# Fixing VectorE's instruction order over the middle stage of a decoder trunk: one step of convolution, recurrence or block sums behind each product's sums

## Chip, cores and metric

The kernel runs on one core of a Trainium2 chip. The metric is device time in microseconds (us), lower is better. The engines named below are PE (TensorE), DVE (VectorE), ACT (ScalarE), POOL (GpSimd) and SP (SyncE, which issues the DMA transfers).

## The reference

One decoder layer for 1024 tokens of width 1024 in float32. The part that matters here is the token-mixing sub-layer: one wide projection `u = h @ w_in` gives the inputs of three branches and their gates, and one of the branches is a recurrence over the tokens.

```python
u = h @ w_in[l]
dq, dk, dv, rq, rk, rv, rg, lx, ly, gates = split(u)
xc = causal_conv4(lx, conv_w) + conv_b            # per channel
r = sigmoid(xc @ w_a + b_a); i = sigmoid(xc @ w_x + b_x)   # 8 blocks of 128
a = exp(-8 * r * softplus(-lam))
b = sqrt(1 - a * a) * (i * xc)
hl[t] = a[t] * hl[t - 1] + b[t]                   # the recurrence (scan)
o_l = hl * gelu(ly)
o_r = silu(rg) * retention_output
merged = sum over 3 branches of sigmoid(gate_i) * (o_i @ w_branch[i])
```

After it come the output projection, cross-attention and the MLP.

## The kernel before

Every float32 operand is split into a high and a low part (`split`, L68: ACT casts the high part, DVE or POOL subtracts to get the low part), and each product is three matmuls (`mm3`). The large products use a seven-product block scheme: a weight pair is two units of 128 output channels, halved into blocks A11 to A22; DVE forms four sums of blocks (`left`, L1115) and two low parts (`prepare` for k = 1, 2), POOL the other five low parts; the right side is the blocks of h. One pair is seven products (`ORDER` = 1, 2, 6, 7, 5, 4, 3, called slots 0 to 6 here) of 12 matmuls into one PSUM tile each; `product` (L1161) then adds the PSUM results into the four output blocks, which is seven PSUM reads by DVE and one copy by ACT. PSUM holds six such tiles (`bufs=6`). `self.line` is a queue of preparations: each product first calls `ahead`, which prepares the unit of the product three further on.

The change is in `h_products` (L647). It goes through 23 pairs: pairs 2, 4, ..., 16 are the eight LRU blocks (`lx` and `ly`), between them stand two `rg` pairs (3 and 5) and then gate pairs. Around an LRU pair p:

- `lru_conv` is four DVE steps over 1024 elements, after slot 5 of pair p;
- `lru_split` and `lru_gate` follow in slots 5 and 6 of pair p + 1: the gate's 12 matmuls write `psr` and `psi`, ACT makes the sigmoids into tiles `r` and `g`, POOL multiplies, ACT does tanh, exp and sqrt, and DVE does four recurrence steps (L638 to L641; the third is the scan);
- `o_sums` loads two row blocks of a branch's output into tiles that share the tags `r` and `g`, makes four subtractions on DVE, and stores them for the next stage. Pair 4 has one set of these sums, pairs 6, 8, 10 and 14 have two, pair 12 one, pairs 18 and 20 one.

Tiles `r` and `g` have one buffer each. So the order of use is gate, recurrence, sums (twice in pairs with two sets), next gate, and each waits until the one before has let go: the sums' load waits for the scan and the last step, the second set's load for the first set's stores to land, and the next sigmoids for the last set's stores.

Nothing fixes the order on DVE except the data and a few `after` chains: a planner places every instruction on its engine by program order and its own estimate of when operands are ready. On the chip each engine then runs its list in that order.

Of the kernel before, what the change touches and what calls it, by code (L numbers as in the profile page):

```python
# [2 lines left out]

# [6 lines left out]
F32 = mybir.dt.float32  # L10
F32R = mybir.dt.float32r
AF = mybir.ActivationFunctionType
ALU = mybir.AluOpType
# [4 lines left out]
P = 128  # L18
S = 1024
D = 1024  # L20
KT = 8
HB = 512
# [5 lines left out]
V_CW = 1  # L28
V_CB = V_CW + 32
# [10 lines left out]
class Split:  # L40


    def __init__(self, hi, lo):
        self.hi, self.lo = hi, lo
# [2 lines left out]
        return Split(self.hi[key], self.lo[key])  # L47


class Kernel:  # L50
    def __init__(self, tc, a, out, ctx):
        self.tc, self.nc, self.a, self.out, self.ctx = tc, tc.nc, a, out, ctx
        self.last, self.put_off, self.filled = {}, [], None
        self.sp = self.sps = None

# [550 lines left out]
        self.split(s, st, self.nc.gpsimd)  # L606
        return s[:, 0, :], s[:, 1, :]

    def lru_conv(self, n, c, sp):
        nc, lx = self.nc, c["lx"]  # L610
        col = lambda base, t=0: self.vec[:, base + 8 * t + n:base + 8 * t + n + 1]
        xc = c["xc"] = sp.tile([P, S], F32, tag="xc", name="xc")
        nc.vector.tensor_scalar(xc, lx[:, 0:S], col(V_CW, 0), col(V_CB), op0=ALU.mult, op1=ALU.add)
        for t in range(1, 4):
            nc.vector.scalar_tensor_tensor(xc, lx[:, t:t + S], col(V_CW, t), xc, op0=ALU.mult, op1=ALU.add)

    def lru_split(self, c):
        xs = self.wpool.tile([P, 2, S], F32R, tag="w", name="xcs")
# [3 lines left out]
    def lru_gate(self, n, c, sp, sps):  # L622
        nc = self.nc
        col = lambda base: self.vec[:, base + n:base + n + 1]
        lw = self.lru_weights(n, sp)
        xc, gy, xs = c["xc"], c["gy"], c["xs"]
        r, g = (sp.tile([P, S], F32, tag=t, name=t) for t in "rg")
        for dst, w, vb in ((r, lw[0], V_BA), (g, lw[1], V_BX)):
            for half in range(2):
                sl = slice(half * HB, (half + 1) * HB)  # L630
                ps = self.ps.tile([P, HB], F32, tag="mm", name="psr") if dst is r else sps.tile([P, HB], F32, tag="p", name="psi", bufs=6)
                self.mm3(ps, w, xs[:, sl], True, True)
                nc.scalar.activation(dst[:, sl], ps, AF.Sigmoid, bias=col(vb))
        nc.gpsimd.tensor_tensor(xc, g, xc, op=ALU.mult)
        nc.scalar.activation(g, r, AF.Tanh, scale=self.sp4[:, n:n + 1])
        nc.scalar.activation(r, r, AF.Exp, scale=self.spm8[:, n:n + 1])
        nc.scalar.activation(g, g, AF.Sqrt)
        nc.vector.scalar_tensor_tensor(g, r, 1.0, g, op0=ALU.add, op1=ALU.mult)  # L638
        nc.vector.tensor_tensor(xc, xc, g, op=ALU.mult)
        nc.vector.tensor_tensor_scan(g, r, xc, 0.0, op0=ALU.mult, op1=ALU.add)  # L640
        nc.vector.tensor_tensor(gy, gy, g, op=ALU.mult)  # L641
        nc.sync.dma_start(self.olT[n * P:(n + 1) * P, :], gy)

    def l4(self, sp):
        return sp.tile([P, S], F32, tag="l4", name="l4", bufs=3)
# [1 line left out]
    def h_products(self):  # L647


        nc, v, a = self.nc, self.nc.vector, self.a  # L650
# [3 lines left out]
        jobs = [("rg", n) for n in range(4)] + [("gate", n) for n in range(self.n_gates, 24, 2)]  # L654
        for n in range(8):
            jobs.insert(2 + 2 * n, ("lru", n))
        cs, m = [{} for _ in jobs], len(jobs)

        sums = {4: [(0, 0)], 6: [(1, 0), (1, 1)], 8: [(1, 2), (1, 3)], 10: [(0, 1), (0, 2)], 12: [(0, 3)],
                14: [(2, 0), (2, 1)], 18: [(2, 2)], 20: [(2, 3)]}  # L660
# [4 lines left out]
        self.bcs = [[{} for _ in range(4)] for _ in range(3)]  # L665
        for i, b in zip((1, 0, 2), self.bcs):
            pairs += [(b[p], [a["w_br"][i * 8 + 2 * p + e] for e in range(2)]) for p in range(4)]

        def prep(p, k):
            self.pair_load(p, *pairs[p])  # L670
            self.prepare(k, pairs[p][0], v if p >= m and k in (6, 4) else nc.gpsimd)

            turns = [x for x in (0, m - 2, m + 2, m + 6, m + 10) if x <= p < x + 2]
            q, at = (p + 1, 6) if not turns else (turns[0] + 2, 3 if p > 1 else 4)
            if k == at and p == (turns or [p])[0] and q < len(pairs):
                self.pair_load(q, *pairs[q])
# [8 lines left out]
        def run(p, k):  # L685
            (kind, n), c, sp, sps = jobs[p], cs[p], self.sp, self.sps
            self.ahead()
            if kind == "lru" and k == 1:
                c["lx"], c["gy"] = sp.tile([P, S + 3], F32, tag="lx", name="lx"), self.l4(sp)
                nc.gpsimd.memset(c["lx"][:, 0:3], 0.0)  # L690

            def emit(i, j, x, y):
                tt = lambda o, x, y, op=ALU.add: v.tensor_tensor(o, x, y, op=op)
                sl = slice(j * HB, (j + 1) * HB)
                if kind == "lru":
                    if i == 1:
                        tt(c["lx"][:, 3 + j * HB:3 + (j + 1) * HB], x, y)
                    else:
                        tt(c["gy"][:, sl], x, y)
                        nc.scalar.activation(c["gy"][:, sl], c["gy"][:, sl], AF.Gelu_apprx_tanh)  # L700
                    return
                o = self.l4(sp)
                row = slice((2 * n + i) * P, (2 * n + i + 1) * P)
                if kind == "gate":
                    g = self.gate_order[n + i]
                    tt(o[:, 0:HB], x, y)
                    nc.sync.dma_start(self.gsp[g * P:(g + 1) * P, sl], o[:, 0:HB])
                else:
                    nc.sync.dma_start(o[:, HB:], self.onT[row, sl])
                    tt(o[:, 0:HB], x, y)  # L710
                    nc.scalar.activation(o[:, 0:HB], o[:, 0:HB], AF.Silu)
                    tt(o[:, 0:HB], o[:, 0:HB], o[:, HB:], ALU.mult)
                    nc.sync.dma_start(self.orT[row, sl], o[:, 0:HB])

            psum = (lambda: self.ps.tile([P, HB], F32, tag="mm", name="ps1")) if k == 1 and p < 2 else None
            self.product(k, c, H, psum or self.p6(sps), emit)
            if kind == "lru" and k == self.ORDER[5]:
                self.lru_conv(n, c, sp)
            if p == 1 and k == 3:
                self.softplus()  # L720
            if p > 0 and jobs[p - 1][0] == "lru":
                if k == self.ORDER[5]:
                    self.lru_split(cs[p - 1])
                elif k == self.ORDER[6]:
                    self.lru_gate(jobs[p - 1][1], cs[p - 1], sp, sps)
            if k == self.ORDER[2]:
                for i, q in sums.get(p, ()):
                    self.o_sums(i, q, sp)

        for p in range(2):  # L730
            run(p, 1)
            yield
# [6 lines left out]
        for k in self.H_FIRST[1:]:  # L739
            for p in range(2):  # L740
                run(p, k)
        for p in range(2, m - 2):
            for k in self.ORDER:
                run(p, k)
        self.right, load = self.load_blocks(1)
        for i, k in enumerate(self.ORDER):
            run(m - 2, k)
# [8 lines left out]
    def o_sums(self, i, q, sp):  # L756

        nc, src, dst = self.nc, self.o_in(i), self.oTs[i]
        t = [sp.tile([P, 2, HB], F32, tag=t, name=t) for t in "rg"]
        for e in range(2):  # L760
            r = (2 * q + e) * P
            self.after("hdma", nc.sync.dma_start(t[e], src[r:r + P, :].rearrange("p (j c) -> p j c", j=2)))
        (b11, b12), (b21, b22) = ([x[:, j, :] for j in range(2)] for x in t)
        for o, x, y in ((b11, b12, b11), (b12, b22, b12), (b22, b22, b11), (b21, b21, b22)):
            nc.vector.tensor_tensor(o, x, y, op=ALU.subtract)
        for e in range(2):
            nc.sync.dma_start(dst[2 * e:2 * e + 2, :, q, :].rearrange("i p c -> p i c"), t[e])

    def o_in(self, i):
        return (self.odT, self.orT, self.olT)[i]  # L770
# [693 lines left out]
```

## Time and profile before

| | us |
|---|---|
| median of three runs (2420.59 to 2424.95) | 2422.93 |
| the profiled execution | 2424.15 |
| its span, first to last instruction | 2422.4 |

| engine | busy us | share of the span |
|---|---|---|
| PE | 2319.7 | 96% |
| DVE | 1888.0 | 78% |
| ACT | 1041.4 | 43% |
| POOL | 955.9 | 39% |

A busy time is a union over the whole span, through stages with different limits. The stretch in which the change's LRU pairs run is read window by window below, from 821 to 1147 us. A window here runs from the first `psr` matmul of one gate to that of the next.

### The profile page before, as it was taken

What the parts mean: (1) busy time and instruction counts of PE and PEld (TensorE: products, weight loads), DVE (VectorE), ACT (ScalarE), POOL (GpSimd) and SP (SyncE); (2) the same over time, 40 slices, a digit from 0 to 9 for tenths busy, and PEclk for the clock granted to TensorE, in tenths of its full rate; (3) what the DMA queues carried; (4) which work ended last, traced back from release to release, by engine and by line L of the source; (5) the groups of instructions that cost most, each with busy time, mean ns of one, the idle gap of its engine ahead of it and who ended that gap; (6) DMA issues with size and microseconds to landing.
All of it is one profiled execution on the core that took longest, in us unless ns stands there. A gap on an engine that the chain in (4) does not pass through costs nothing. (4 is left out here: it accounts for less than half of the span.)

```text
span 2422.4 us, 31108 instructions
## 1 busy us (share of the span) xinstructions
PE 2319.7 (96%) x11156; PEld 1913.1 (79%) x11156; DVE 1888.0 (78%) x2909; ACT 1041.4 (43%) x1817; POOL 955.9 (39%) x621
## 2 busy tenths in 40 slices
PE   9999999999999998999999988999989999899998
PEld 7888878888887876777887767778768888788886
DVE  7677487878797788798787898344788888788896
ACT  5443355555555543554354444135442222343333
POOL 1122212222215444455431223034155555598863
PEclk9999999999999999999999999999999999999999
DMA  5222122222215354543576687343225443744341
GB/s 173 81 87 70 58 70 60 64 71 70 62 49 180 127 162 162 174 134 136 178 266 240 228 287 239 105 146 119 97 83 183 152 144 135 254 167 166 121 165 70
DMA packets 135994, 335.12 MB, mean 138 GB/s; under 512 B 17040, under 2 KB 27281, under 8 KB 135840
## 3 DMA queue, kind: packets, MB, share of 16 engines
q1 hardware_dynamic: 135264, 331.30, 41.4%
q8 instruction: 89, 1.46, 0.2%
q10 hardware_dynamic: 576, 1.84, 0.2%
q14 instruction: 65, 0.53, 0.1%
HBM read 227.64 MB, written 97.05 MB: 134 GB/s over the span
## 5 line engine op out<-in xcount | busy, mean ns | idle before, releaser
L59 PE MATMUL ps<-block,wu 128*128 128x512 f32 x1428 | 568.6, 398 | 27.2 <-DVE sf L1187 10.4
L61 PE MATMUL ps<-block,wu 128*128 128x512 f32 x1428 | 565.3, 396 | 10.2 <-DVE wu L71 10.2
L60 PE MATMUL ps<-block,wu 128*128 128x512 f32 x1428 | 561.9, 394 | 0.8 <-DVE block L71 0.8
L71 POOL TENSOR_TENSOR wu<-st,wu 128x512 fp32r<-128x512 f32 x144 | 227.3, 1585 | 303.4 <-ACT wu L70 290.4
L59 PEld LDWEIGHTS ps<-block,wu 128*128 128x128 f32 x1428 | 272.4, 191 | 89.0 <-DVE sf L1187 11.3
L61 PEld LDWEIGHTS ps<-block,wu 128*128 128x128 f32 x1428 | 271.2, 190 | 75.1 <-DVE wu L71 13.3
L60 PEld LDWEIGHTS ps<-block,wu 128*128 128x128 f32 x1428 | 271.8, 190 | 61.0 <-DVE block L71 1.3
L70 ACT CAST wu<-st 128x512 fp32r<-128x512 f32 x240 | 141.9, 620 | 210.1 <-DVE st L1117 94.1
L71 POOL TENSOR_TENSOR w<-st,w 128x1024 fp32r<-128x1024 f32 x50 | 124.6, 2501 | 176.7 <-ACT w L70 176.5
L59 PE MATMUL ps<-wu,hu 128*128 128x512 f32 x456 | 179.4, 394 | 8.0 <-ACT wu L70 4.2
L60 PE MATMUL ps<-wu,hu 128*128 128x512 f32 x456 | 178.9, 392 | 0.9 <-POOL wu L71 0.8
L61 PE MATMUL ps<-wu,hu 128*128 128x512 f32 x456 | 178.6, 392 | 0.0
L71 POOL TENSOR_TENSOR wu<-sf,wu 128x512 fp32r<-128x512 f32 x63 | 122.2, 1954 | 131.9 <-ACT wu L70 95.8
L1273 DVE TENSOR_TENSOR acc<-acc,ps 128x512 f32<-128x512 f32 x184 | 118.1, 679 | 19.8 <-PE ps L61 19.4
L71 DVE TENSOR_TENSOR hu<-sth,hu 128x1024 fp32r<-128x1024 f32 x53 | 118.1, 2231 | 14.3 <-ACT hu L70 13.6
L466 ACT ACTIVATE p<-sc,mx 128x256 f32<-128x256 f32 (+7 forms) x128 | 94.8, 742 | 69.9 <-DVE mx L463 50.1
L71 DVE TENSOR_TENSOR wu<-st,wu 128x512 fp32r<-128x512 f32 x96 | 91.1, 960 | 30.9 <-ACT wu L70 30.8
L59 PEld LDWEIGHTS ps<-wu,hu 128*128 128x128 f32 x456 | 86.3, 189 | 28.7 <-ACT wu L70 4.6
L59 PE MATMUL psk<-block,w 128*128 128x512 f32 x256 | 101.6, 397 | 0.0
L60 PEld LDWEIGHTS ps<-wu,hu 128*128 128x128 f32 x456 | 86.3, 189 | 19.3 <-POOL wu L71 1.3
L61 PE MATMUL psk<-block,w 128*128 128x512 f32 x256 | 101.2, 395 | 0.0
L60 PE MATMUL psk<-block,w 128*128 128x512 f32 x256 | 100.8, 394 | 0.0
(383 smaller groups left out, 5627.4 us busy)
## 6 DMA issues: line engine op xcount, KB each, us to landing
sth<-h SPq DMA_DIRECT2D x53, 512.0 KB, 3.2
st<-in_w SPq DMA_DIRECT2D x32, 512.0 KB, 4.2
h<-hab SPq DMA_DIRECT2D x32, 512.0 KB, 2.8
w<-in_w SPq DMA_DIRECT2D x8, 2048.0 KB
block<-oTs SPq DMA_DIRECT2D x24, 512.0 KB, 5.8
sgb<-gsp SPq DMA_DIRECT2D x48, 256.0 KB, 5.3
gsp<-l SPq DMA_DIRECT2D x44, 256.0 KB, 2.8
acc<-y SPq DMA_DIRECT2D x40, 256.0 KB, 2.9
```

Of the source, the lines that this page charges most:

```text
L59: nc.tensor.matmul(ps, lhsT=lhs.hi, rhs=rhs.hi, start=start, stop=False)
L60: nc.tensor.matmul(ps, lhsT=lhs.hi, rhs=rhs.lo, start=False, stop=False)
L61: nc.tensor.matmul(ps, lhsT=lhs.lo, rhs=rhs.hi, start=False, stop=stop)
L70: ins = self.nc.scalar.copy(dst.hi, src)
L71: self.lo_ins = (lo_engine or self.nc.vector).tensor_tensor(dst.lo, src, f32(dst.hi), op=ALU.subtract)
L466: nc.scalar.activation(p[:, 0:n], sc[:, 0:n], AF.Exp, bias=mx, accum_out=l)
L1273: v.tensor_tensor(acc[k][:, st, :], acc[k][:, st, :], ps, op=ALU.add)
```

## The change

DVE's instructions in pairs 2 to 20 are chained in program order (`in_order`, key `"dve"`), so that the planner can no longer move them against each other, and the program order itself is rewritten: behind each product's sums stands one step. For an LRU pair p: convolution in slots 5 and 6 of p and 0 and 1 of p + 1, split in slot 2, gate in slot 4 of p + 1, recurrence in slots 1 to 4 of p + 2. The first set of block sums is loaded in slot 4 of an LRU pair. A second set is loaded in slot 0 of the next pair and subtracted in its slots 2 and 3. The `rg` pairs' last multiplication is put off by one product. No arithmetic is added or taken away.

```diff
+class InOrder:
+    def __getattr__(self, name):
+        def issue(*args, **kw):
+            ins = getattr(self.engine, name)(*args, **kw)
+            if self.kernel.in_order:
+                self.kernel.after("dve", ins)
+            return ins
+        return issue
...
-    def lru_conv(self, n, c, sp):
+    def lru_conv(self, n, c, sp, t):
...
+        if t == 0:
+            c["xc"] = sp.tile([P, S], F32, tag="xc", name="xc")
+            nc.vector.tensor_scalar(c["xc"], lx[:, 0:S], col(V_CW, 0), col(V_CB), op0=ALU.mult, op1=ALU.add)
+        else:
+            nc.vector.scalar_tensor_tensor(c["xc"], lx[:, t:t + S], col(V_CW, t), c["xc"], op0=ALU.mult, op1=ALU.add)
...
+    def lru_scan(self, n, c, step):
+        v, xc, gy, (r, g) = self.nc.vector, c["xc"], c["gy"], c["rg"]
+        if step == 0:
+            v.scalar_tensor_tensor(g, r, 1.0, g, op0=ALU.add, op1=ALU.mult)
+        elif step == 1:
+            v.tensor_tensor(xc, xc, g, op=ALU.mult)
+        elif step == 2:
+            v.tensor_tensor_scan(g, r, xc, 0.0, op0=ALU.mult, op1=ALU.add)
+        else:
+            v.tensor_tensor(gy, gy, g, op=ALU.mult)
+            self.nc.sync.dma_start(self.olT[n * P:(n + 1) * P, :], gy)
...
+                    def gated(o=o, row=row, sl=sl):
+                        tt(o[:, 0:HB], o[:, 0:HB], o[:, HB:], ALU.mult)
+                        nc.sync.dma_start(self.orT[row, sl], o[:, 0:HB])
+                    puts.append([2, gated])
...
+            for x in puts:
+                x[0] -= 1
+            while puts and puts[0][0] == 0:
+                puts.popleft()[1]()
+
+            at = self.ORDER.index(k)
+            lru = lambda q: 0 <= q < m and jobs[q][0] == "lru"
+            if lru(p - 2) and 0 < at < 5:
+                self.lru_scan(jobs[p - 2][1], cs[p - 2], at - 1)
+            if lru(p) and at > 4:
+                self.lru_conv(n, c, sp, at - 5)
+            if lru(p - 1):
+                if at < 2:
+                    self.lru_conv(jobs[p - 1][1], cs[p - 1], sp, at + 2)
+                elif at == 2:
                     self.lru_split(cs[p - 1])
-                elif k == self.ORDER[6]:
+                elif at == 4:
                     self.lru_gate(jobs[p - 1][1], cs[p - 1], sp, sps)
-            if k == self.ORDER[2]:
-                for i, q in sums.get(p, ()):
-                    self.o_sums(i, q, sp)
+            if p in sums and at == 4:
+                self.steps = itertools.chain.from_iterable(self.o_sums(i, q, sp) for i, q in sums[p])
+                next(self.steps)
+            if p == m - 3 and p in sums:
+                count = {5: 2, 6: 2}.get(at, 0)
+            elif p in sums:
+                count = len(sums[p]) * (at == 6)
+            elif p < m - 2:
+                count = {0: {1: 1, 2: 3}, 1: {1: 1}, 2: {1: 1, 2: 2}, 3: {2: 2}}.get(at, {}).get(len(sums.get(p - 1, ())), 0)
...
+            for _ in range(count):
+                next(self.steps)
...
+        self.in_order = True
         for p in range(2, m - 2):
             for k in self.ORDER:
                 run(p, k)
+        self.in_order = False
...
         for o, x, y in ((b11, b12, b11), (b12, b22, b12), (b22, b22, b11), (b21, b21, b22)):
+            yield
             nc.vector.tensor_tensor(o, x, y, op=ALU.subtract)
```

## Rows read from the trace of the kernel before

**Rows 1.** The page's first part: busy us of each engine, share of the span, and instructions.

```profile
PE 2319.7 (96%) x11156; PEld 1913.1 (79%) x11156; DVE 1888.0 (78%) x2909; ACT 1041.4 (43%) x1817; POOL 955.9 (39%) x621
```

**Rows 2.** The stretch of the LRU pairs in windows, each from the first `psr` matmul of a gate to that of the next. Columns: window and its length in us, busy us and number of instructions of each engine, granted clock of PE (1.00 is 2.4 GHz), DMA share and rate.

```profile
821.20:862.50 41.30, 41.30 (x182) 33.80 (x180) 32.94 (x36) 24.63 (x34) 19.79 (x12) 1.00 0.46 152
862.50:907.50 45.00, 42.04 (x182) 33.56 (x180) 36.15 (x39) 22.73 (x32) 21.80 (x13) 1.00 0.41 133
907.50:957.50 50.00, 43.40 (x182) 34.53 (x180) 42.18 (x45) 21.98 (x31) 21.97 (x13) 0.97 0.48 167
957.50:1006.20 48.70, 44.81 (x181) 35.92 (x180) 41.84 (x44) 22.10 (x31) 23.23 (x13) 0.93 0.49 165
1006.20:1055.20 49.00, 43.62 (x181) 34.84 (x181) 42.16 (x45) 21.98 (x31) 23.27 (x13) 0.97 0.49 167
1055.20:1098.20 43.00, 41.55 (x182) 33.74 (x181) 39.47 (x43) 23.24 (x33) 23.47 (x14) 1.00 0.46 150
1098.20:1146.90 48.70, 43.60 (x183) 35.04 (x182) 41.53 (x43) 24.46 (x34) 26.59 (x14) 0.96 0.33 114
```

**Rows 3.** Who waited for whom from 862.5 to 1146.9 us. Columns after the releaser: us in total, times, longest.

```profile
PE psr L60 <- DVE xcs L71: 11.0, 6, 2.6
PE ps L59 <- DVE sf L1187: 10.4, 5, 3.6
...
ACT L633 <- DMA oTs<-r: 18.3, 2, 9.2
ACT L633 <- DVE l L693: 17.4, 2, 8.8
```

**Rows 4.** VectorE's timeline, the recurrence's first step (L638) of four LRU blocks: start us, length us, instruction. The last row is that line's summary for all eight: least, median and greatest ns, and the first and last start.

```profile
885.54 1.22 DVE L638 SCALAR_TENSOR_TENSOR g<-r,g 128x1024 f32<-128x1024 f32 x1
...
983.51 1.22 DVE L638 SCALAR_TENSOR_TENSOR g<-r,g 128x1024 f32<-128x1024 f32 x1
...
1032.15 1.22 DVE L638 SCALAR_TENSOR_TENSOR g<-r,g 128x1024 f32<-128x1024 f32 x1
...
1072.96 1.22 DVE L638 SCALAR_TENSOR_TENSOR g<-r,g 128x1024 f32<-128x1024 f32 x1
...
L638 DVE SCALAR_TENSOR_TENSOR g<-r,g x8: 1216/1217/2261, 837.2 to 1161.5; 128x1024 f32<-128x1024 f32 x8
```

**Rows 5.** VectorE's timeline between the second and third of these, in part.

```profile
984.64 0.69 DVE L1184 TENSOR_TENSOR sf<-ps,sf 128x512 f32<-128x512 f32 x1
...
988.08 3.37 DVE L640 TENSOR_TENSOR_SCAN g<-r,xc 128x1024 f32<-128x1024 f32 x1
...
991.96 1.67 DVE L641 TENSOR_TENSOR l<-l,g 128x1024 f32<-128x1024 f32 x1
...
1002.35 1.28 DVE L615 SCALAR_TENSOR_TENSOR xc<-lx,vec,xc 128x1024 f32<-128x1024 f32 x1
1003.54 0.68 DVE L765 TENSOR_TENSOR g<-g 128x512 f32<-128x512 f32 x1
1004.15 0.68 DVE L693 TENSOR_TENSOR l<-ps,sf 128x512 f32<-128x512 f32 x1
...
1013.99 1.75 DVE L765 TENSOR_TENSOR r<-g,r 128x512 f32<-128x512 f32 x1
...
1017.46 0.68 DVE L765 TENSOR_TENSOR g<-g 128x512 f32<-128x512 f32 x1
```

**Rows 6.** ScalarE's timeline over the same stretch, in part; the bracket is the idle time before and what ended it.

```profile
1003.74 1.05 ACT L70 CAST xcs<-xc 128x1024 fp32r<-128x1024 f32 x1 [2.71 <-PE ps L61]
...
1018.68 1.28 ACT L633 ACT_TABLE_LOAD   x1 [9.15 <-DMA oTs<-r]
1019.98 1.27 ACT L633 ACTIVATE r<-psr,vec 128x512 f32<-128x512 f32 x2
...
1030.15 1.06 ACT L637 ACTIVATE g<-g 128x1024 f32<-128x1024 f32 x1
...
1033.07 1.13 ACT L70 CAST wu<-st 128x512 fp32r<-128x512 f32 x2
```

**Rows 7.** SyncE's timeline, issues of the block sums' stores and loads (start us, length of the issue), and under it two rows of the DMA view from 840 to 1160 us: transfers, KB each, median us from issue to landing.

```profile
1004.25 0.38 SPq L767 DMA_DIRECT2D oTs<-g  x1
...
1007.70 0.32 SPq L762 DMA_DIRECT2D g<-odT  x1
...
1018.16 0.37 SPq L767 DMA_DIRECT2D oTs<-g  x1
...
oTs<-g SPq DMA_DIRECT2D x10, 512.0 KB, 2.8
...
g<-odT SPq DMA_DIRECT2D x4, 512.0 KB, 4.4
```

**Rows 8.** Three lines of VectorE from 820 to 1190 us (the last over the whole span): least, median and greatest ns.

```profile
L1182 DVE TENSOR_TENSOR sf<-ps,sf x16: 680/684/686, 836.6 to 1183.3; 128x512 f32<-128x512 f32 x16
...
L1117 DVE TENSOR_TENSOR sf<-sf x8: 684/1765/1776, 864.2 to 1188.1; 128x512 f32<-128x512 f32 x8
...
L613 DVE TENSOR_SCALAR xc<-lx,vec x8: 812/1782/1790, 804.5 to 1134.4; 128x1024 f32<-128x1024 f32 x8
```

**Rows 9.** The gate with one set of sums before it: TensorE's second `psr` matmul, and ScalarE's last activation of that gate (start us, length us).

```profile
1057.05 0.50 PE L60 MATMUL psr<-xcs,lw 128*128 128x512 f32 x1 [1.45 <-DVE xcs L71]
...
1071.04 1.06 ACT L637 ACTIVATE g<-g 128x1024 f32<-128x1024 f32 x1
```

More of the change, by code (lines that the diff above doesn't have):

```diff
@@ L1 @@
 import collections
+import itertools
 from contextlib import ExitStack
@@ L47, in __getitem__, with __init__, __getattr__ @@
         return Split(self.hi[key], self.lo[key])
+class InOrder:
+    def __init__(self, kernel, engine):
+        self.kernel, self.engine = kernel, engine
+    def __getattr__(self, name):
[5 more added lines that the diff above has]
+        return issue
+class Engines:
+    def __init__(self, kernel, nc):
+        self.kernel, self.nc = kernel, nc
+        self.in_order = InOrder(kernel, nc.vector)
+    def __getattr__(self, name):
+        if name == "vector":
+            return self.in_order
+        return getattr(self.nc, name)
 class Kernel:
     def __init__(self, tc, a, out, ctx):
-        self.tc, self.nc, self.a, self.out, self.ctx = tc, tc.nc, a, out, ctx
+        self.tc, self.a, self.out, self.ctx = tc, a, out, ctx
+        self.in_order, self.nc = False, Engines(self, tc.nc)
         self.last, self.put_off, self.filled = {}, [], None
@@ L607, in lru_weights @@
         return s[:, 0, :], s[:, 1, :]
-    def lru_conv(self, n, c, sp):
+    def lru_conv(self, n, c, sp, t):
         nc, lx = self.nc, c["lx"]
         col = lambda base, t=0: self.vec[:, base + 8 * t + n:base + 8 * t + n + 1]
[L612 to L615, printed above, removed]
+        if t == 0:
[3 more added lines that the diff above has]
+            nc.vector.scalar_tensor_tensor(c["xc"], lx[:, t:t + S], col(V_CW, t), c["xc"], op0=ALU.mult, op1=ALU.add)
     def lru_split(self, c):
@@ L637, in lru_gate @@
         nc.scalar.activation(g, g, AF.Sqrt)
[L638 to L642, printed above, removed]
+        c["rg"] = r, g
+    def lru_scan(self, n, c, step):
[9 more added lines that the diff above has]
+            self.nc.sync.dma_start(self.olT[n * P:(n + 1) * P, :], gy)
     def l4(self, sp):
@@ L667, in h_products @@
             pairs += [(b[p], [a["w_br"][i * 8 + 2 * p + e] for e in range(2)]) for p in range(4)]
+        puts = collections.deque()
         def prep(p, k):
@@ L711, in emit @@
                     nc.scalar.activation(o[:, 0:HB], o[:, 0:HB], AF.Silu)
-                    tt(o[:, 0:HB], o[:, 0:HB], o[:, HB:], ALU.mult)
-                    nc.sync.dma_start(self.orT[row, sl], o[:, 0:HB])
+                    def gated(o=o, row=row, sl=sl):
+                        tt(o[:, 0:HB], o[:, 0:HB], o[:, HB:], ALU.mult)
+                        nc.sync.dma_start(self.orT[row, sl], o[:, 0:HB])
+                    puts.append([2, gated])
             psum = (lambda: self.ps.tile([P, HB], F32, tag="mm", name="ps1")) if k == 1 and p < 2 else None
@@ L716, in run @@
             self.product(k, c, H, psum or self.p6(sps), emit)
-            if kind == "lru" and k == self.ORDER[5]:
-                self.lru_conv(n, c, sp)
             if p == 1 and k == 3:
                 self.softplus()
-            if p > 0 and jobs[p - 1][0] == "lru":
-                if k == self.ORDER[5]:
+            for x in puts:
[4 more added lines that the diff above has]
+            lru = lambda q: 0 <= q < m and jobs[q][0] == "lru"
@@ L730, in h_products @@
+            if p == m - 3 and p in sums:
[4 more added lines that the diff above has]
+                count = {0: {1: 1, 2: 3}, 1: {1: 1}, 2: {1: 1, 2: 2}, 3: {2: 2}}.get(at, {}).get(len(sums.get(p - 1, ())), 0)
+            else:
+                count = 0
+            for _ in range(count):
+                next(self.steps)
         for p in range(2):
@@ L767, in o_sums @@
             nc.sync.dma_start(dst[2 * e:2 * e + 2, :, q, :].rearrange("i p c -> p i c"), t[e])
+        yield
     def o_in(self, i):
```

## The prediction

> **What bounds the kernel now.** The page's first part makes PE the bound, 96% busy, with DVE second at 78% [rows 1]; both are averages. So I read the stretch of the LRU pairs in windows of two pairs [rows 2]. The first shows the pace that PE keeps when nothing stops it: 41.3 us for 182 matmuls, all of them busy. The other six sum to 284.4 us where six times 41.3 is 247.8: 36.6 us are lost there, and that is all the change can win. Four windows lose 7.4 to 8.7 us each (50.0, 48.7, 49.0, 48.7); they are those with two sets of block sums. In them DVE is busy 41.9 us on average, already more than PE's 41.3.
>
> The table of waits [rows 3] names the ends of PE's stalls: the low part of `xc` (11.0 us) and PSUM not yet read (10.4). It also shows where delay starts: ACT's sigmoids stood still 35.7 us, in four waits of up to 9.2, two of them until a store of the sums' tile `r` had landed.
>
> That points at tiles `r` and `g`, which have one buffer each: gate, recurrence, sums, second sums, gate. The starts of the recurrence's first step measure this loop [rows 4]. 885.54 to 1032.15 is three loops of 48.9; 837.2 to 885.54 is 48.3; 1032.15 to 1072.96, with one set, is 40.8; the last two together 88.5. All seven take 324.3. A loop with two sets consists of three parts [rows 4 to 6]: on DVE from the first step (983.51) to the end of the last subtraction (1017.46 plus 0.60: 1018.06), 34.55 us; then store, sigmoids, tanh, exp and sqrt up to ACT's end at 1031.21, 13.15; then 0.94 until DVE begins. So the question is not whether DVE's work is spread, but what stands on DVE between the first step and the last subtraction.
>
> **The change, part by part.** Prices are from start to start [rows 4, 5]: a 512-element operation 0.60 us (1003.54 to 1004.15), a 1024-element one 1.13 (983.51 to 984.64), a convolution step 1.19 (1002.35 to 1003.54), the scan 3.3 and the last recurrence step 1.6 (their lengths less 0.07), the convolution's first step 1.7 (length 1.78 in the median) [rows 8].
>
> *Spreading and chaining.* By the new program order DVE does between these two points, in slots 1 to 6 of the LRU pair and 0 to 3 of the next: nine PSUM reads (5.4), two low parts and four block sums of a weight pair (3.6), eight subtractions (4.8), four convolution steps (1.7 and 3 x 1.19: 5.3), four recurrence steps (7.15), the low part of `xc` (1.1). Sum 27.4. Counted in the same way the old stretch holds ten PSUM reads and eight weight operations, else the same: 29.2. Of its 34.55 us some 5.3 are stretching beyond these prices.
>
> *Stretching.* Additions that read PSUM take 680 to 686 ns whatever else runs; one that reads SBUF alone is 684 at least and 1765 in the median [rows 8], so up to 1.1 us longer beside POOL. Eight POOL splits fall into the new stretch: bounds 0 and 8.8 us on 27.4. Each step now stands behind a PSUM read, during which a POOL operation that is running gets on; I take 3.5, somewhat less than the 5.3 of now.
>
> *New waits, and what queues behind them.* First, the low part of `xc` waits for ACT's cast of 1.05 [rows 6], which starts when the last convolution step ends; one PSUM read (0.60) covers part: 0.55 is left. Second, the second sums' `g`: from the end of the first set (1004.15) to the issue of `g`'s next load (1007.70) passed 3.55, and a load takes 4.4 [rows 5, 7], so `g` is there 8.0 after the first set. Before, the second subtraction began only 9.8 after it (1013.99) and waited for nothing. Now only a PSUM read, a convolution step, another read, the cast wait, the low part and one subtraction stand between, 4.7 to 5.5; DVE would wait 2.5 to 3.3, bounds 0 (if stretching fills it) and 3.3; I take 3.0. Behind it queue the rest of the sums, the next weight's low part and all PSUM reads, for which PE waits.
>
> *Gate earlier.* It moves from slot 6 to 4, past two products. With two sets this gives nothing, since the sigmoids wait for the sums' stores. The last subtraction now comes nearer behind the second, which holds `r`'s store, so the part after it grows by about 0.5 to 13.65.
>
> *Put-off multiplication, wrappers, queues.* The same instructions and transfers. SP's loads keep their places relative to the steps that free their tiles. Cost nothing while the silu and load of an `rg` output hide under the next product.
>
> **The sum.** Two sets: 27.4 + 3.5 + 0.55 + 3.0 + 13.65 + 0.1 = 48.2 (bounds 41.7 and 53.5: stretching 0 and 8.8, `g` 0 and 3.3, the part after it 13.15 to 13.65; PE's 41.3 hardly enters). Before, the four took 195.5 (three of 48.9; of the last two's 88.5, 48.9): now 192.8. One set: from the first step to the end of `xc`'s low part 23.8 by the same prices, 0.55 and 3 of stretching: 27.4. From there, PE's second gate matmul (1057.05) to the end of sqrt (1072.10) is 15.05 [rows 9]. 42.4 in all, 1.6 more than the 40.8 now, because the old order had its convolution done sooner. The first loop, with `rg`: its sigmoids now stand ahead of the last two outputs' silu; 42.4 plus 2.6 of put-off work, 45.0, 3.3 less. The last, without sums: PE's pace, 41.3 for 39.6. Total 45.0 + 192.8 + 42.4 + 41.3 = 321.5 for 324.3: 2.8 less. The profiled execution took 2424.15, 1.2 above the median of its runs (2422.93), so 2421.35 becomes 2420 us. A change of 0.2% (4.8 us) is about what a measurement here can tell from none.
>
> **The rivals.** *The loop shortens.* Half the stretching (1.75) and half the wait (1.5) go: 45.0 per loop with two sets, 12.8 less in four, 2407. For it: the steps really are apart from one another; against: the same eight POOL splits meet them.
>
> *Cured.* All seven loops at PE's pace: 289.1 for 324.3, 35.2 less, 2388. Against it: DVE's 41.9 busy.
>
> *Slower: a cast behind the gate's chain.* When the recurrence starts, ACT's next casts of weight blocks come behind the sqrt (1033.07) [rows 6]. In the new order the next pair's block sums stand in one piece in slot 5, late. If the planner puts the third unit's cast behind sqrt, its POOL part ends some 2.5 later, its product takes 2.7 (12 of 182 matmuls in 41.3) and the PSUM read in front of the second recurrence step, 1.1 after the first began, finds nothing: about 3.9 us more per loop with two sets. It decides as soon as that unit is ready later than 1.6 before the sqrt ends. 52.1 per loop, 15.6 more: 2436.
>
> *Slower: the port.* If every one of the eight POOL splits stretches a DVE operation by the full 1.1, the loop is 53.5 less the `g` wait that stretching fills (2 of 3.3), 51.5; four times 3.3 more, 2433.
>
> The Trainium skill speaks for this last one: "SBUF — State Buffer", under "Who interferes with whom", says that a VectorE instruction with two SBUF inputs contends with a GpSimd instruction that reads SBUF, and that the later of the two blocks fully. By that rule alone a step put behind each product meets a POOL split in nearly every slot. Rows 8 agree on the kind: only the SBUF form is stretched.
>
> **How the numbers follow.** Loop about as long as now, 0.45 (2413 to 2427 on its own: 0.10 faster by over 0.2%, 0.35 within); shorter 0.25; cured 0.06; cast 0.14; port 0.10. Faster 0.41, same 0.35, slower 0.24. From 2404 to 2436 the range leaves out the cure and about half of the worst: under 2 in 10.
>
> **What would show it.** The first-step starts: 48 apart with two sets if I am right, 45 or 41 if not. ACT's wait ahead of the sigmoids should be some 5 us, DVE's new wait on the load of `g` 2 to 3. If neither is there and windows of 49 became 42, the loop argument is wrong; if PE waits for weights at slot 2 of an LRU pair, it is the cast.

## The result, and the profile after

The changed kernel takes 2433.17 us (median of five runs, 2426.10 to 2433.34) beside 2422.93 for the kernel before. The ratio is 1.0038, 95% interval 1.0024 to 1.0051: slower by 0.38%, 9 us or so. The time lies inside the forecast range, but on the other side of no change than the 2420 that was forecast. The profiled execution's span is 2430.9 us, 8.5 more than before.

First the page's busy line of the kernel after, beside [rows 1]:

```profile
PE 2324.2 (96%) x11156; PEld 1913.0 (79%) x11156; DVE 1852.1 (76%) x2909; ACT 1048.1 (43%) x1825; POOL 950.8 (39%) x621
```

DVE runs the same 2909 instructions in 35.9 us less, and the kernel is slower. So DVE's busy time isn't the explanation. The windows of the LRU stretch come next, cut from gate to gate as in [rows 2]; the columns are those of that group.

```profile
816.12:861.41 45.29, 41.97 (x181) 33.46 (x180) 34.17 (x39) 28.12 (x37) 21.08 (x12) 1.00 0.39 136
861.41:912.49 51.08, 45.26 (x180) 35.36 (x180) 38.37 (x45) 29.09 (x39) 23.32 (x13) 0.93 0.43 139
912.49:961.15 48.66, 42.53 (x181) 33.47 (x181) 37.28 (x44) 21.96 (x32) 20.74 (x13) 1.00 0.47 165
961.15:1012.09 50.94, 44.26 (x181) 34.17 (x181) 37.71 (x44) 21.95 (x32) 20.49 (x13) 0.97 0.46 156
1012.09:1059.59 47.50, 43.88 (x181) 34.57 (x181) 36.99 (x43) 21.95 (x32) 21.06 (x13) 0.96 0.45 162
1059.59:1105.11 45.52, 43.05 (x180) 34.71 (x181) 35.68 (x41) 22.16 (x32) 19.80 (x13) 0.96 0.43 139
1105.11:1153.12 48.01, 43.72 (x180) 34.71 (x181) 34.27 (x40) 22.03 (x32) 21.43 (x12) 0.96 0.35 124
```

The seven windows sum to 337.0 where before they took 325.7 [rows 2]. In the four behind two sets (the third, fourth, fifth and last) DVE is busy 36.6 us on average where it was 41.9, yet they are only 1.3 us shorter in sum; the other three take 12.6 more. Since the gate's place moved from slot 6 to slot 4, the cuts lie elsewhere in a pair, and the loops are the better measure.

The starts of the recurrence's first step, read one by one from VectorE's timeline, are 835.55, 884.59, 934.52, 985.49, 1034.36, 1079.52, 1129.63 and 1171.29. The loops between them, beside the forecast and with four of the experiments (told below), are:

| kernel | first, with `rg` | two sets (mean of four) | one set | last, no sums | sum |
|---|---|---|---|---|---|
| before | 48.4 | 48.9 | 40.8 | 39.6 | 324.3 |
| forecast for after | 45.0 | 48.2 | 42.4 | 41.3 | 321.5 |
| after | 49.0 | 50.0 | 45.2 | 41.7 | 335.7 |
| after, stores first | 47.7 | 48.6 | 43.5 | 41.6 | 327.1 |
| after, copy on DVE | 49.7 | 49.9 | 43.3 | 39.5 | 332.3 |
| after, both of these | 47.0 | 49.1 | 41.0 | 39.5 | 323.8 |
| after, no chain | 45.5 | 48.8 | 38.2 | 40.1 | 319.1 |

Loops 11.4 us longer than before account for the slowdown. The first loop begins 1.6 us earlier than before and 4.2 are lost between the last first step and the branch stage, the stage that comes next, so its first load is issued 14.0 us later (1228.1 for 1214.1). Of these 14.0 the rest of the kernel wins 5.5 back. No edit in this document is aimed at that rest, and from the first branch load to the end of the span it takes between 1197.7 and 1209.1 us in the profiles here. Whole times that differ by a few us therefore say less of the stretch than the loops do.

One two-set loop step by step, as it was taken apart in the prediction. VectorE's timeline of the kernel after (start us, length us, instruction; the bracket is the idle time before and what ended it):

```profile
985.49 1.23 DVE L59 SCALAR_TENSOR_TENSOR g<-r,g 128x1024 f32<-128x1024 f32 x1 [6.76 <-ACT g L667]
...
1003.09 1.78 DVE L59 TENSOR_TENSOR r<-r 128x512 f32<-128x512 f32 x1
1004.90 1.67 DVE L59 TENSOR_TENSOR r<-g,r 128x512 f32<-128x512 f32 x1
...
1012.07 1.23 DVE L59 TENSOR_TENSOR xcs<-xc,xcs 128x1024 fp32r<-128x1024 f32 x1 [0.59 <-ACT xcs L98]
1014.26 0.72 DVE L59 TENSOR_TENSOR r<-r 128x512 f32<-128x512 f32 x1 [0.96 <-DMA r<-odT]
1016.19 0.69 DVE L59 TENSOR_TENSOR r<-g,r 128x512 f32<-128x512 f32 x1 [1.21 <-DMA g<-odT]
...
1018.12 1.12 DVE L59 TENSOR_TENSOR g<-g 128x512 f32<-128x512 f32 x1
1019.16 0.68 DVE L59 TENSOR_TENSOR wu<-st,wu 128x512 fp32r<-128x512 f32 x1
...
1034.36 1.23 DVE L59 SCALAR_TENSOR_TENSOR g<-r,g 128x1024 f32<-128x1024 f32 x1 [5.95 <-ACT g L667]
```

DVE's part, from 985.49 to the end of the last subtraction, where the next instruction starts (1019.16), is 33.7 us where the forecast had 34.45. The rest is 15.2 where it had 13.75. ScalarE in the same kernel and stretch:

```profile
1021.61 1.28 ACT L663 ACT_TABLE_LOAD   x1 [4.23 <-DMA oTs<-r]
...
1033.27 1.06 ACT L667 ACTIVATE g<-g 128x1024 f32<-128x1024 f32 x1
```

And SyncE's issues, first of the kernel before, then of the kernel after:

```profile
997.72 0.33 SPq L1128 DMA_DIRECT2D st<-in_w_gate  x1
998.10 0.42 SPq L1128 DMA_DIRECT2D sf<-in_w_gate  x1
...
1015.76 0.37 SPq L767 DMA_DIRECT2D oTs<-r  x1
```

```profile
1014.46 0.33 SPq L1198 DMA_DIRECT2D st<-in_w_gate  x1
1014.84 0.42 SPq L1198 DMA_DIRECT2D sf<-in_w_gate  x1
1016.91 0.38 SPq L836 DMA_DIRECT2D oTs<-r  x1
```

Before, the next pair's weights (two transfers of 512 KB) were issued 18.0 and 17.7 us ahead of `r`'s last store, and the sigmoids' table load began 2.9 after that store's issue [rows 6]. After, they are issued 2.5 and 2.1 us ahead of it, and the table load begins 4.7 after the store's issue. Over the four loops with two sets this distance is 4.3, 6.3, 4.7 and 6.6 us, where it was 2.9 to 3.0 in each before. Two rows of the DMA view from 840 to 1160 us (transfers, KB each, median us from issue to landing) say the same of the stores: `r` before, where [rows 7] has 2.8 for `g` as well, then both after.

```profile
oTs<-r SPq DMA_DIRECT2D x10, 512.0 KB, 2.8
```

```profile
oTs<-r SPq DMA_DIRECT2D x10, 512.0 KB, 4.4
oTs<-g SPq DMA_DIRECT2D x10, 512.0 KB, 3.3
```

What released these loads can be read too. A load of weights waits until POOL has read the staging tile for a low part. First POOL of the kernel before, then ACT and POOL of the kernel after:

```profile
996.07 1.62 POOL L71 TENSOR_TENSOR wu<-st,wu 128x512 fp32r<-128x512 f32 x1 [1.28 <-ACT wu L70]
```

```profile
1010.99 1.04 ACT L98 CAST xcs<-xc 128x1024 fp32r<-128x1024 f32 x1 [8.81 <-DVE xc L59]
1011.94 1.65 ACT L98 CAST wu<-st 128x512 fp32r<-128x512 f32 x3
```

```profile
1012.64 1.79 POOL L99 TENSOR_TENSOR wu<-st,wu 128x512 fp32r<-128x512 f32 x1 [1.60 <-ACT wu L98]
```

In both kernels the load is issued 0.03 us after this low part ends (997.69 and 997.72; 1014.43 and 1014.46). In the kernel after, the cast that the low part needs stands in ACT's list behind the cast of `xc`, and that one waits 8.8 us for the last convolution step, which DVE's fixed order has put behind a product of the next pair. The other three loops with two sets show the same chain, with waits of 8.3 to 8.8.

The waits of the kernel after from 861.4 to 1153.1 us (us in total, times, longest):

```profile
ACT L663 <- DMA oTs<-r: 22.6, 4, 7.3
DVE l L59 <- ACT sf L1248: 15.9, 4, 7.7
...
DVE l L59 <- ACT l L752: 7.9, 1, 7.9
```

The wait on `r`'s store now stands ahead of all four gates that follow two sets. Two waits of DVE on ACT are new or nearly so: on a copy out of PSUM (L1248), and on a silu (L752), for which DVE waited 0.7 us before. Both stand in ACT's list behind the square root; here they are in the first loop, ScalarE of the kernel after, and VectorE behind it:

```profile
879.96 1.06 ACT L667 ACTIVATE g<-g 128x1024 f32<-128x1024 f32 x1
881.03 1.28 ACT L752 ACT_TABLE_LOAD   x1
882.33 0.63 ACT L752 ACTIVATE l<-l 128x512 f32<-128x512 f32 x1
...
883.37 0.58 ACT L1248 COPY sf<-ps 128x512 f32<-128x512 f32 x1
```

```profile
882.99 0.69 DVE L59 TENSOR_TENSOR l<-l 128x512 f32<-128x512 f32 x1 [7.94 <-ACT l L752]
883.98 0.69 DVE L59 TENSOR_TENSOR l<-ps,sf 128x512 f32<-128x512 f32 x1 [0.30 <-ACT sf L1248]
884.59 1.32 DVE L59 SCALAR_TENSOR_TENSOR g<-r,g 128x1024 f32<-128x1024 f32 x1
```

The square root ends at 881.02 and the recurrence could begin. In the fixed order, though, its first step stands behind an addition that needs the copy and the multiplication that needs the silu, and it begins 3.6 us later.

### The profile page after: what moved, and what is told of

The parts are those of the page before. It is cut to its first block, busy times and chain, and to the rows that moved or that the text cites. A ratio compares the mean times of both kernels' runs of the same rounds, so it can differ in the third digit from the quotient of the medians.

```text
span 2430.9 us, 31118 instructions
## 1 busy us (share of the span) xinstructions
PE 2324.2 (96%) x11156; PEld 1913.0 (79%) x11156; DVE 1852.1 (76%) x2909; ACT 1048.1 (43%) x1825; POOL 950.8 (39%) x621
## 3 DMA queue, kind: packets, MB, share of 16 engines
q1 hardware_dynamic: 135264, 331.30, 41.2%
## 5 line engine op out<-in xcount | busy, mean ns | idle before, releaser
L89 PE MATMUL ps<-block,wu 128*128 128x512 f32 x1428 | 566.1, 396 | 16.7 <-POOL wu L99 11.3
L99 POOL TENSOR_TENSOR wu<-st,wu 128x512 fp32r<-128x512 f32 x144 | 232.3, 1621 | 318.4 <-ACT wu L98 298.9
L87 PEld LDWEIGHTS ps<-block,wu 128*128 128x128 f32 x1428 | 271.9, 190 | 83.4 <-ACT wu L98 18.4
L99 POOL TENSOR_TENSOR wu<-sf,wu 128x512 fp32r<-128x512 f32 x63 | 113.5, 1817 | 114.4 <-ACT wu L98 86.9
L59 DVE TENSOR_TENSOR acc<-acc,ps 128x512 f32<-128x512 f32 x200 | 128.3, 677 | 19.7 <-PE ps L89 19.5
L87 PEld LDWEIGHTS ps<-wu,hu 128*128 128x128 f32 x456 | 86.0, 189 | 26.6 <-DVE hab L59 3.5
L88 PEld LDWEIGHTS ps<-wu,hu 128*128 128x128 f32 x456 | 86.0, 189 | 19.5 <-POOL wu L99 1.4
L89 PEld LDWEIGHTS ps<-wu,hu 128*128 128x128 f32 x456 | 86.0, 189 | 17.8
```

The costliest lines, as they stand in the source:

```text
L59: ins = getattr(self.engine, name)(*args, **kw)
L87: nc.tensor.matmul(ps, lhsT=lhs.hi, rhs=rhs.hi, start=start, stop=False)
L88: nc.tensor.matmul(ps, lhsT=lhs.hi, rhs=rhs.lo, start=False, stop=False)
L89: nc.tensor.matmul(ps, lhsT=lhs.lo, rhs=rhs.hi, start=False, stop=stop)
L99: self.lo_ins = (lo_engine or self.nc.vector).tensor_tensor(dst.lo, src, f32(dst.hi), op=ALU.subtract)
```

## The experiments

Theory A: the loop through tiles `r` and `g` sets the stretch's time, and the new order lengthens it where the sums' last store meets the weight loads. Theory B: the chain itself costs, since DVE may not step past an addition whose operand ACT makes late. They don't exclude each other; the runs price them. Each ratio is against runs of the kernel before measured with that experiment: its median was 2422.07 for runs 1 to 4, 2419.34 for 5, 7 and 8, and 2422.41 for 6, 9 and 10.

**1. The new program order without the chain.**

```diff
-        self.in_order = True
+        self.in_order = False
```

> The changed kernel with its new program order, but without the chain on VectorE. Loop theory (time goes by the length of the loop gate, recurrence, sums, second sums, gate through the one-buffer tiles r and g): the planner keeps most of the new order, so the loops with two sets stay at 49 to 51 us, 2428 to 2436. Rival (the chain itself costs, by VectorE's strict waits for ACT's copy and casts): without it the 10 us come back, 2418 to 2425.

Measured 2420.96 us beside 2422.07 for before, ratio 0.9986 (0.9973 to 0.9999). The chain costs some 12 us over the same program order, as the rival had it. That doesn't yet tell the theories apart: without the chain DVE makes the last convolution step sooner too, and in the loop that answers to the one above the weights are issued 9.0 and 7.3 us ahead of `r`'s store and the table load begins 2.8 after it. The planner left to itself gives the first loop 45.5 and the one-set loop 38.2. ScalarE of this kernel, in the first loop:

```profile
874.46 0.62 ACT L752 ACTIVATE l<-l 128x512 f32<-128x512 f32 x1
...
878.83 1.06 ACT L667 ACTIVATE g<-g 128x1024 f32<-128x1024 f32 x1
879.80 0.57 ACT L1248 COPY sf<-ps 128x512 f32<-128x512 f32 x1
```

The silu stands ahead of the square root, the copy still behind it; but DVE began the recurrence at 879.93, where the square root ends, and made the addition that needs the copy later.

**2. The chain alone, on the old program order.** The kernel before with `in_order` set over pairs 2 to 20, and nothing else.

> The kernel before with VectorE chained in its old program order over pairs 2 to 20. There the four recurrence steps stand right behind the gate, so VectorE must stand still for the whole of ACT's sigmoid, tanh, exp and sqrt (some 12 to 15 us) in each of eight LRU blocks. Loop theory: that wait lies on the loop with all else behind it, 6 to 10 us more per LRU block, 2470 to 2510. Rival (a fixed order as such costs little, PSUM covers the wait): 2423 to 2435.

Measured 2513.4, ratio 1.0373 (1.0350 to 1.0397), just above the range. The loops sum to 404.6, 80 more than before. A chain over an order that was written for a planner is costly; the new order takes most of that back, but not all.

**3. Fewer sums in a loop, on the kernel before.**

```diff
-        sums = {4: [(0, 0)], 6: [(1, 0), (1, 1)], 8: [(1, 2), (1, 3)], 10: [(0, 1), (0, 2)], 12: [(0, 3)],
-                14: [(2, 0), (2, 1)], 18: [(2, 2)], 20: [(2, 3)]}
+        sums = {4: [(0, 0)], 6: [(1, 0)], 8: [(1, 1)], 10: [(1, 2)], 12: [(1, 3)], 14: [(0, 1)], 16: [(2, 0)],
+                18: [(2, 1), (2, 2)], 19: [(0, 2), (0, 3)], 20: [(2, 3)]}
```

> The kernel before with the sets of block sums dealt out otherwise: one set per LRU pair from 4 to 16, and two, two and one in pairs 18, 19 and 20, where no gate follows. The same arithmetic. Loop theory: the four loops with two sets (49 us) become loops with one (41 us), 4 x 8 = 32 less, 2388 to 2398. Rival (VectorE's total work in a window is the limit, 41.9 of 41.3 us, or PSUM reads behind the scan): little is won, 2415 to 2425.

Measured 2403.71, ratio 0.9919 (0.9890 to 0.9948). The loops are 48.3, then 40.9 to 42.2, in sum 296.6: 27.7 less than before. With one set to a loop they run at PE's pace of [rows 2], as the loop theory has it. The run lightens DVE as well, though: the stretch now holds seven sets and not ten, 12 subtractions fewer. What speaks against DVE's total work as the limit is the kernel after, whose windows behind two sets last 48.8 us with DVE busy for 36.6. The time falls by only 18.4. The rest is lost behind the last LRU pair, where five sets now lie on three pairs (run 9).

**4. The sums' stores ahead of the loads, on the kernel after.** The stores are put into the chain that keeps SP's weight loads in order.

```diff
-            nc.sync.dma_start(dst[2 * e:2 * e + 2, :, q, :].rearrange("i p c -> p i c"), t[e])
+            self.after("wdma", nc.sync.dma_start(dst[2 * e:2 * e + 2, :, q, :].rearrange("i p c -> p i c"), t[e]))
```

> The changed kernel with the stores of the block sums put in one chain with the weight loads on SP's queue, in program order, so that the second set's stores are issued ahead of the next pair's 1 MB of weights and not behind. Loop theory, with the store as the mis-sized term: r's store lands in 2.9 us again where it took 4.6 to 6.5, so each loop with two sets is 1.5 to 3.5 us shorter, 2421 to 2427. Rival (the store's landing is hidden, VectorE's waits decide): 2431 to 2435.

Measured 2421.38, ratio 0.9997 (0.9982 to 1.0011): in the time the slowdown is gone. In the stretch it isn't quite: the loops sum to 327.1, 8.6 less than after and 2.8 more than before, and the first branch load is issued at 1219.1, 9.0 earlier than after and 5.0 later than before. The rest of the gain lies behind that load and isn't explained. SyncE, and ScalarE's table load, of the loop that answers to the one above:

```profile
1013.47 0.33 SPq L633 DMA_DIRECT2D lws<-in_w_la  x1
1013.91 0.38 SPq L836 DMA_DIRECT2D oTs<-r  x1
...
1016.32 0.80 SPq L1198 DMA_DIRECT2D st<-in_w_gate  x1
1017.17 0.64 SPq L1198 DMA_DIRECT2D sf<-in_w_gate  x1
```

```profile
1016.94 1.28 ACT L663 ACT_TABLE_LOAD   x1 [4.40 <-DMA oTs<-r]
```

Store to table load is 3.0 us again, and the median landing of `oTs<-r` in the stretch is 2.7. The two-set loops come down to 48.6 on average. The one shown is the exception: it went from 48.9 to 49.7, since `r` was ready at 1011.64 but its store was issued only at 1013.91, behind a load of the gate's weights (`lws`) in SP's list. The other three lost 1.3, 2.4 and 2.7.

**5. The copy out of PSUM on DVE instead of ACT while the chain is on, on the kernel after.**

```diff
-            nc.scalar.copy(t0, c[1])
+            (nc.vector.tensor_copy if self.in_order else nc.scalar.copy)(t0, c[1])
```

> The kernel after with the copy of a product's second sum out of PSUM on DVE instead of ACT while the chain is on. If DVE's ordered stream loses time because that copy stands behind the square root in ACT's queue (22.9 us of such waits between 820 and 1200), the first, the one-set and the last loop shorten by 1 to 2 us each and the two-set ones by nothing: 2426 to 2431. Rival: the store's landing alone sets the loops, and the copies are only more work for DVE (about 100 of them of 0.5 us): 2433 to 2442.

Measured 2428.41, ratio 1.0035 (1.0022 to 1.0047), which can't be told from after's 1.0038. In the loops it did what theory B says for the one-set loop (1.9 us shorter) and the last (2.1), not for the first (0.7 longer); in the time nothing of it is left. The rival's price was too high: 19 copies moved to DVE, of 0.68 us each, not about 100.

**6. Both mends, 4 and 5.**

> The kernel after with both mends: the sums' stores ahead of the next loads, and the copy out of PSUM on DVE while the chain is on. If what is left of the chain's cost after the first mend (loops of 327 in sum, against 319 without the chain) is that copy behind the square root in ACT's queue, the loops sum to 319 to 323 and the time is 2413 to 2419. If the silu behind the square root and DVE's fixed order around it are left, 324 to 327 and 2419 to 2424.

Measured 2424.22, ratio 1.0004 (0.9994 to 1.0013). The loops sum to 323.8, 0.5 less than before, and the time is that of before. The part of the chain's cost that is left against run 1 (4.7 us of loops) lies in neither of the two mends. In the first loop DVE still waits for the silu; what makes up the rest isn't settled. The start of the first branch load, where all that happened in the stretch is summed up, gives the shares: 1228.1 after, 1219.1 with the stores first, 1225.7 with the copy, 1216.0 with both, 1213.3 without the chain (1214.1 before). Of 14.8 us the stores give back 9.0, both mends 12.1.

**7. Fewer sums in a loop, on the kernel after.** The deal of run 3, chain on.

> The kernel after with the block sums dealt out one set to a pair instead of two (pairs 6 to 16), the last five on the pairs 18 to 20; the chain stays. If the loop from one pair's step 0 to the next is what the four two-set pairs pay for (two sets of subtractions, their reload and two stores ahead of the gate), those loops fall from 49 to 51 us to about 43 to 45, the last one rises by 1 to 3, and the time goes to 2405 to 2422, some 10 us of it given back by the pairs 18 to 20 as in the same deal on the kernel before. Rival: the chain's waits on ACT (silu and copy queued behind sqrt) set the loops whatever the sums do: loops stay at 47 or above and the time at 2428 to 2436.

Measured 2427.23, ratio 1.0029 (1.0018 to 1.0040). Neither theory's number: the loops fell as theory A has it (43.4 to 45.9 with one set, in sum 313.3, 22.4 less than after), but the time did not. The first block load of the branch stage shows where it went. SyncE's issues of these loads, one summary line each for before, after and this kernel (least, median and greatest ns, first and last start):

```profile
L791 SPq DMA_DIRECT2D block<-orT x6: 359/414/462, 1214.1 to 1252.9; - x6
```

```profile
L861 SPq DMA_DIRECT2D block<-orT x6: 360/424/868, 1228.1 to 1266.8; - x6
```

```profile
L860 SPq DMA_DIRECT2D block<-orT x6: 359/428/1111, 1220.3 to 1260.8; - x6
```

The last first step of the recurrence is at 1161.48, 1171.29 and 1148.86. So the way from there to the branch stage is 52.6, 56.8 and 71.4 us: of the 22.4 us won in the loops 14.6 go into the way past the five sets on pairs 18 to 20. Of the 7.8 that are left at the first branch load the span keeps 4.0; where the others go isn't shown.

**8. Fewer sums in a loop and stores first; fewer sums in a loop without the chain** (on the kernel after).

> The kernel after with both: one set to a pair, and the sums' stores ahead of the next pair's weight loads in SP's list. If the two causes stand behind one another (fewer sums, and stores that land at once), it is faster than the spread alone by 2 to 6 us: 2400 to 2418. Rival: with one set the store has time to land behind the loads, and the two come out the same within 2 us.

> The program order of after with the spread sums but without the chain on DVE. If the chain costs some 12 us on top of the new order (as without the spread), it is 5 to 12 us faster than the chain with the spread: 2396 to 2412, loops near 41. Rival: the chain's cost lay in the two-set pairs alone, and both come out the same within 3 us.

Measured 2412.25 (0.9971, interval 0.9960 to 0.9983) and 2410.51 (0.9965, 0.9952 to 0.9978), against 2427.23 for the chain with the deal alone: 15.0 and 16.7 us less, where at most 6 and 12 had been expected. The late store costs more than that with one set as well: there it is `g`'s store that lands late, 4.9 us in the median and 3.5 with the stores first, and the loops fall from 313.3 to 304.2. Without the chain they are 302.6. With the stores first, most of what the chain cost is gone.

**9. The five last sets spread too, on the kernel before.**

```diff
-                18: [(2, 1), (2, 2)], 19: [(0, 2), (0, 3)], 20: [(2, 3)]}
+                18: [(2, 1)], 19: [(2, 2)], 20: [(2, 3)], 21: [(0, 2)], 22: [(0, 3)]}
```

> The kernel before with one set of block sums to each of the pairs 4 to 22, so that the five sets that the earlier deal put on the pairs 18 to 20 go to 18 to 22. If what that deal gave back after its last LRU pair (the first block load 15 to 17 us later behind the last step 0 than where two sets lie there) is the crowd of sets on 18 to 20, half of it or more comes back: 2392 to 2400. Rival: the branch stage's loads need the sums that now come last, and wait for them, or the crowd is only moved to the pairs 21 and 22: 2401 to 2412.

Measured 2397.77, ratio 0.9897 (0.9882 to 0.9912), the lowest time here, 1% below before. SyncE's branch loads of run 3 and of this kernel:

```profile
L791 SPq DMA_DIRECT2D block<-orT x6: 385/451/592, 1196.0 to 1236.7; - x6
```

```profile
L791 SPq DMA_DIRECT2D block<-orT x6: 379/498/820, 1187.1 to 1228.8; - x6
```

The last first steps are at 1132.7 and 1133.5; the way to the branch stage is 63.3 us in run 3 and 53.6 here, 52.6 in the kernel before. So the crowd on pairs 18 to 20 was what lengthened that way. The intervals of the two times overlap, so that the later deal is faster than run 3 rests on these traces (the first branch load 8.9 us earlier), not on the times.

**10. Stores first on the kernel before**, with the deals of runs 9 and 3.

> The same deal, and the sums' stores put ahead of the next weight loads in SP's list. If a store that lands late holds the loop of the kernel before too (its r landed 4.3 us after issue with one set to a pair, 2.8 with two), 2 to 8 us faster than without; if only the chain makes DVE reach its stores late, no difference within 2 us.

> The spread of the earlier run (five sets on the pairs 18 to 20) on the kernel before, with the stores ahead of the loads. The same two answers as for the later deal: 2396 to 2402 if the late store holds the loop, 2402 to 2406 if it doesn't.

Measured 2455.75 (1.0142, 1.0125 to 1.0159) and 2471.32 (1.0205, 1.0184 to 1.0225): 58 and 68 us slower than without, the opposite of both answers that I had put down. SyncE of the second, and the row of its waits (820 to 1160 us) that stands out:

```profile
1003.75 0.37 SPq L767 DMA_DIRECT2D oTs<-r  x1
...
1008.82 1.34 SPq L1128 DMA_DIRECT2D st<-in_w_lru  x2
```

```profile
ACT wu L70 <- DMA st<-in_w_lru: 68.6, 6, 13.4
```

The edit that ties stores and loads together here pulls the loads behind the stores, and ACT waits up to 13.4 us for weights. In the kernel after the loads stood 2 us ahead of the store anyway, so they lost little by the same edit. What was right to mend there was the order at one meeting point, not stores ahead of loads as such.

## Why the prediction was wrong

**DVE's part of the loop: right.** 34.45 forecast, 33.7 measured in the loop above. The wait for the cast was 0.59 (0.55), the waits for the reloaded tiles 0.96 and 1.21, together 2.2 for 3.0. That step held. (The bounds given for such a loop are slightly off by their own terms: 41.7 and 53.5 should be 41.2 and 53.8.)

**Stretching: right in sum, partly by luck, and the port rival refuted.** 33.7 less 27.4, 0.6 and 2.2 leaves the 3.5 that was taken. The items differ. The prices of the scan, the last recurrence step and the first convolution step, taken from stretched rows, were 1.6 too high together, and five instructions took 4.1 more than theirs: two subtractions of the first set (1.78 and 1.67), the last subtraction (1.12), a low part and a convolution step. One group of additions that read SBUF alone had taken 1765 ns in the median [rows 8]. Now, by the same summary for the kernel after, 820 to 1190 us:

```profile
L59 DVE TENSOR_TENSOR sf<-sf x8: 676/678/679, 846.9 to 1181.0; 128x512 f32<-128x512 f32 x8
```

All eight are at the short value; in this kernel it is the subtractions on `r` that are stretched (1306 ns on average, 849 before). The port rival's 8.8 us isn't there in the loop shown, and DVE's busy time fell by 35.9 us. The rival's time, 2433, is the one that was measured, but by another mechanism: the number agrees by chance.

**The part after the last subtraction: the step that failed.** The forecast gave it 13.65 because it let the sigmoids start 2.9 us behind `r`'s store as before. What failed is how one sentence was used: "SP's loads keep their places relative to the steps that free their tiles." Taken by its words it holds, since the load still follows POOL's low part by 0.03 us. But the forecast took it to mean that the loads keep their place relative to the store too, and costed that at nothing. The low part itself moved, behind the cast of `xc`, and relative to the last store of `r` the loads moved from 17.7 us ahead to 2.1. The store then lands behind 1 MB of loads: 5.5 us from its issue to the table load on average over the four loops, 2.5 more than before. The loops with two sets miss their forecast by 1.75 each, 7.1 of the 14.2 us by which the sum of the loops misses. Run 4 mends this alone, and the two-set loops are then 48.6 for a forecast of 48.2. That its time is 2421 for a forecast of 2420 is chance in part: its loops sum to 327.1 for 321.5, and the difference is won behind the stretch.

**The first loop: wrong by 4.0 (45.0 forecast, 49.0 measured).** The forecast put the gate's sigmoids ahead of the last silu, counted 2.6 of put-off work, and costed the put-off multiplication at nothing "while the silu hides under the next product". In ACT's list the silu and the copy stand behind the square root, so the multiplication and an addition hold the recurrence in DVE's fixed order. Without the chain the loop took 45.5, and 49.0 less the 3.6 us after the square root is 45.4. **The one-set loop: wrong by 2.8** (42.4, measured 45.2). The stores first take 1.7 of it away and the copy 1.9, both together 4.2. **The last: 41.3 forecast, 41.7 measured**, though with the copy on DVE it is 39.5, as before.

**The cast rival: the right kind, another instruction.** It had DVE's order held by work queued on ACT behind the gate's chain, at the third unit's cast and in the two-set loops. What stands there is the silu and the copy, in the first, the one-set and the last loops (at the end of the one-set loop DVE waits 7.7 us for the copy, of the last 6.7). The two-set loops begin their recurrence right at the square root's end (1033.27 plus 1.06, and 1034.36).

**ACT's wait** ahead of the sigmoids was to be "some 5": 4.2 in the loop shown, 5.7 on average over the four. It looked like a confirmation, but the wait counts from ACT's last work, not from the store's issue, and so it hid that the store had become slower.

**The cured rival** needed PE's pace in all loops, and it was refused because DVE's busy time stood at 41.9. Run 3 comes to 296.6 in an unfixed order, with three sets fewer in the stretch. DVE was not full at 41.9 in a window of 49; the loop through `r` and `g` held it.

## What to carry to other kernels

Where a tile is used in a ring, measure that ring start to start, and ask of each transfer in it what else is issued on its queue shortly before: an order fixed on one engine moves the transfers of others past each other. A fixed order on DVE has to be laid against the lists of the engines that feed it, since one late copy then holds everything behind it. And spread the work that goes through the ring over more turns before ordering the work inside one; here the first gave 25 us and the second lost about 10.

## What the runs showed of the hardware that was not expected

A store of 512 KB that landed 2.8 us after its issue in the median took 4.4 in the median, and up to 6.6 to the wait that it ended, when two loads of 512 KB were issued on the same queue 2 to 3 us ahead of it; with the store issued first it was 2.7 again.

How much DVE's additions from SBUF are stretched beside POOL depends on where the order puts them, instruction by instruction: one group went from 1765 ns in the median to 678, another from 849 on average to 1306, with 2909 instructions on DVE and 621 on POOL in both kernels. From 820 to 1190 us, of the additions and subtractions of 512 elements with both operands in SBUF that have a row to themselves in VectorE's timeline, 69 of 143 overlapped a POOL instruction before (by over 0.1 us) and 39 of 144 after. None of the others took more than 0.69 us in either kernel; of those that overlapped, 49 and 28 took more than 0.75. The Trainium skill, "SBUF — State Buffer", "Who interferes with whom", has the rule that such an instruction contends with a GpSimd one that reads SBUF. These counts agree with it; how many such meetings an order brings, no count of instructions told.
